# FFN1 of four tiles in pairs, x resident between statistics and normalization, split rings for x, and h2 held on chip, in a Hymba-style decoder layer

## Chip, cores and metric

One Trainium2 chip, eight cores. Each core computes four of the 32 sequences, with no exchange between cores. The time of a run is the device time of the slowest core. "A die" is cores 0 to 3 or cores 4 to 7. Some executions fell into a slow state, in which one die or both were granted a lower TensorE clock (in the kernel before, medians of 0.80 to 0.91 on the worse die, against 0.92 to 0.93 in its fast runs).

## The reference, cut to what matters

```python
h = h + 0.5 * swiglu(rmsnorm(h, g_ffn1), w_ffn1_gate, w_ffn1_up, w_ffn1_down)   # FFN1 -> h1
u = rmsnorm(h, g_mix)
proj = u @ w_in                                                                # the mixer:
o = concat(rmsnorm(mla_group(...)), rmsnorm(swa_group(...)))                   # two attention groups
h = h + o @ w_o                                                                # -> h2
h = h + 0.5 * swiglu(rmsnorm(h, g_ffn2), w_ffn2_gate, w_ffn2_up, w_ffn2_down)   # FFN2
return rmsnorm(h, g_final)
```

D_MODEL is 1024, D_FF 2816. A core works on 16 tiles of 512 tokens, features on the partitions, so a tile of x, h1 or h2 is eight blocks of 128x512 float32, 256 KB each (2.1 MB).

## The kernel before

The program writes its operations in any order, each with a priority `v`. A list scheduler with a model of durations then fixes the order of every engine, and semaphores follow from the data. So the order on an engine is fixed before the run. Four streams are interleaved: FFN1 and FFN2 tile by tile, the mixer of one tile spread between them, and at the start the "background", which converts the weights of the mixer and FFN2 from float32 to bf16 in device memory. FFN1's weights are converted while the first two tiles ("J") use them.

```python
NX = 3
X = [sb(f"X{i}", [128, T], F32)[0] for i in range(NX)]      # one ring for x, h1 and h2
...
phases = [("J", 0, 2 * ff)]                                  # tiles 0 and 1 share each weight piece
for n in range(2, look): phases.append(("F1", n, ff))        # look = 4
for n in range(1, NT + 1):
    phases.append(("F2", n - 1, ff))
    if n + look - 1 < NT: phases.append(("F1", n + look - 1, ff))
...
def load_x(src, key, dv=-8.0):
    i, t = xr.next()
    k.dma(f"x{i}", t[:], src, ...)
...
if ph == "F1":                                               # x twice through the ring
    sc.v = vmap(f0 - 45.0); x_stats(n, rsF)                  # 8 loads, squares, sum on GpSimd
    sc.v = vmap(f0 - 20.0); make_uF(n, uF, rsF)              # 8 loads, uF = x * g * rs
...
# end of the mixer
    i, t = load_x(h1_s[n, dc], ("h1", n, dc))
    k.tt("dve", t[:], PS[bk][:], t[:], ALU.add)              # h2
    st.add(t[:])
    k.dma(f"xs{i}", h2_s[n, dc], t[:], ...)
for c in range(8):
    _, t = load_x(h2_s[n, c], ("h2", n, c))                  # h2 again, for FFN2
    k.stt(uF[:, c, :], t[:], gcol("f2", c), rsH[:], ALU.mult, ALU.mult)
```

FFN1 and FFN2 have a gate/up phase G (352 matmuls of 128x128x512 a tile) and a down phase D (176). A "round" is FFN2 of one tile, FFN1 of another and a mixer; there are twelve, then a tail of FFN2 and mixers without FFN1.

The softmax here doesn't subtract the row's maximum and nothing guards it: scores larger than these inputs give would overflow.

## Time and profile before

| | before |
|---|---|
| median of 3 first runs | 6023.84 us (6017.51 to 6049.1) |
| profiled fast run | 6063 us on its slowest core (core 5) |
| FFN2 of tile 0 starts (core 5) | 837 us |
| a round, mean of twelve | 359.5 us |
| tail, from FFN2 of tile 12 on | 912 us |
| bytes moved | 1083.54 MB |

The prediction shows the lines. They are read thus: in the view by stretches the share of PE busy time says how full the bounding engine is, and the granted clock says what its work cost; matmuls times 0.206 us (the price in a phase without waits at clock 1.00) is what the stretch would need. The rest is loss. The 0.61, 0.54 and 1.00 that the prediction sets side by side are granted clocks of its views; its half clock is a granted 0.50, as the trace of this run (core 5) has it from 456 to 504 us (8 matmuls, PE busy for 3.9 us) and from 2442 to 2458, in the gap of 21.7 us. In the waits, sb_uF is the normalized input of an FFN, sb_sqb the sum of squares that the statistics matmul reads, sb_W a weight piece, sb_tb the buffers of the tanh chain; sb_stJ and sb_stB are the staging buffers of FFN1's weights and of the background, sb_obB the background's converted pieces.

### The profile page before, as it was taken

The page shows a single profiled execution, that of the slowest core. Times are in us where ns is not written, and L with a number is a line of the kernel's source. Part 1 is how long each engine was busy: PE and PEld are TensorE (multiplying, and loading weights), DVE is VectorE, ACT ScalarE, POOL GpSimd, SP SyncE. Part 2 cuts the span into 40 slices and gives each one's busy share as a digit, 9 for nine tenths or more (in the row PEclk, how much of TensorE's full clock was granted, in tenths as well). Part 3 has the DMA queues.
Part 4 walks back from the last instruction along what each step waited for, and adds up shares of the span by engine and source line. Part 5 has one row for each costly group of instructions (what it writes and reads, how often), then busy time and mean ns, then how long its engine had stood idle before and what let it go on. Part 6 is the DMA issues. An engine that isn't in the chain of part 4 may idle for free.

```text
span 6063.0 us, 78231 instructions; the slowest of 8 cores (5933.8 to 6063.0 us)
## 1 busy us (share of the span) xinstructions
PE 5233.1 (86%) x23152; PEld 2234.1 (37%) x23152; DVE 2374.5 (39%) x3418; ACT 2514.0 (41%) x4215; POOL 1222.3 (20%) x1511
## 2 busy tenths in 40 slices
PE   1976889899898899889898888989989889889878
PEld 0422334343333334334343333434334343334333
DVE  0313434435434444533435353343533444443432
ACT  1102424445353433525455242434535343646551
POOL 3441212111111211212111121211111121121210
PEclk9988899999998999999999999999999999989887
DMA  9996565644545555564644656555464555463534
GB/s 277 302 307 188 163 211 169 193 157 154 192 151 187 169 186 169 159 205 152 184 144 132 209 165 211 169 188 161 148 199 151 186 170 187 134 195 117 156 117 138
DMA packets 426072, 1083.54 MB, mean 179 GB/s; under 512 B 47424, under 2 KB 52032, under 8 KB 425536
## 3 DMA queue, kind: packets, MB, share of 16 engines
q1 hardware_dynamic: 425664, 1078.54, 56.3%
q8 instruction: 202, 3.31, 0.2%
q14 instruction: 206, 1.69, 0.1%
HBM read 933.52 MB, written 144.83 MB: 178 GB/s over the span
## 4 chain that ended last, share of the span: by engine, by line
PE 61%; DMA 23%; DVE 5%; ACT 4%; issue 3%; POOL 2%; SPq 2%; DVEq 0%; ACTq 0%; POOLq 0%
PE ps L315 61%; DMA sb_stB_100<-wgu 2%; SPq L364 2%; DMA sb_X_63<-h2s 2%; DMA h1s<-sb_X_63 2%; DMA sb_X_62<-xT 2%; DMA sb_X_62<-h1s 2%; DMA h1s<-sb_X_62 1%; DMA sb_X_61<-h1s 1%; DMA sb_X_63<-h1s 1%; DMA sb_X_63<-xT 1%; DMA h2s<-sb_X_61 1%; DMA h2s<-sb_X_62 1%; DVE sb_HB L340 1%; DMA sb_X_61<-xT 1%
## 5 line engine op out<-in xcount | busy, mean ns | idle before, releaser
L315 PE MATMUL ps<-sb_uF,sb_W_66 128*128 128x512 bf16 x2720 | 684.0, 397 | 160.7 <-DVE sb_uF L340 137.6
L315 PE MATMUL ps<-sb_uF,sb_W_64 128*128 128x512 bf16 x2736 | 672.6, 389 | 79.4 <-DVE sb_uF L340 74.3
L315 PE MATMUL ps<-sb_uF,sb_W_65 128*128 128x512 bf16 x2736 | 661.6, 389 | 49.6 <-DVE sb_tb_78 L340 40.0
L315 PE MATMUL ps<-sb_uF,sb_W_67 128*128 128x512 bf16 x2720 | 661.2, 393 | 30.1 <-POOL sb_W_67 L334 8.5
L323 ACT ACT_TABLE_LOAD x269 | 345.1, 1283 | 458.1 <-PE ps L315 444.1
L315 PE MATMUL ps<-sb_QT,sb_KT 96*128 96x512 bf16 (+3 forms) x1280 | 434.2, 369 | 78.9 <-ACT sb_PT_75 L323 19.7
L340 DVE SCALAR_TENSOR_TENSOR sb_tb_78<-sb_tb_78,ps 128x512 f32<-128x512 f32 x352 | 241.7, 687 | 607.8 <-ACT sb_tb_78 L323 607.3
L315 PEld LDWEIGHTS ps<-sb_uF,sb_W_66 128*128 128x128 bf16 x2720 | 266.9, 100 | 524.3 <-issue 249.1
L340 DVE SCALAR_TENSOR_TENSOR sb_tb_79<-sb_tb_79,ps 128x512 f32<-128x512 f32 x352 | 241.6, 686 | 550.6 <-ACT sb_tb_79 L323 549.5
L315 PEld LDWEIGHTS ps<-sb_uF,sb_W_64 128*128 128x128 bf16 x2736 | 266.3, 99 | 427.4 <-issue 143.0
L323 ACT ACTIVATE sb_tb_79<-ps 128x512 f32<-128x512 f32 x352 | 210.1, 597 | 504.9 <-PE ps L315 503.7
L315 PEld LDWEIGHTS ps<-sb_uF,sb_W_65 128*128 128x128 bf16 x2736 | 267.7, 99 | 391.6 <-issue 108.0
L315 PEld LDWEIGHTS ps<-sb_uF,sb_W_67 128*128 128x128 bf16 x2720 | 269.8, 100 | 378.8 <-issue 95.8
L323 ACT ACTIVATE sb_tb_78<-ps 128x512 f32<-128x512 f32 x352 | 210.1, 597 | 473.1 <-PE ps L315 471.9
L315 PE MATMUL ps<-sb_act,sb_W_66 128*128 128x512 bf16 x1364 | 338.1, 392 | 18.8 <-DVE sb_X_63 L340 8.5
L315 PE MATMUL ps<-sb_act,sb_W_65 128*128 128x512 bf16 x1364 | 329.2, 389 | 19.2 <-DMA sb_W_65<-wd1s 13.1
L315 PE MATMUL ps<-sb_act,sb_W_67 128*128 128x512 bf16 x1364 | 327.3, 388 | 20.0 <-POOL sb_W_67 L334 15.8
L315 PE MATMUL ps<-sb_act,sb_W_64 128*128 128x512 bf16 x1364 | 331.6, 385 | 14.6 <-DMA sb_W_64<-wd1s 8.1
L348 POOL TENSOR_TENSOR sb_sqa_83<-sb_sqa_83,sb_sq_81 128x512 f32<-128x512 f32 x88 | 112.0, 1272 | 964.8 <-ACT sb_sq_81 L323 963.3
L348 DVE TENSOR_TENSOR sb_act<-sb_tb_78,ps 128x512 bf16<-128x512 f32 x352 | 241.4, 686 | 144.7 <-PE ps L315 139.8
L348 POOL TENSOR_TENSOR sb_sqa_82<-sb_sqa_82,sb_sq_80 128x512 f32<-128x512 f32 x139 | 183.0, 1317 | 531.0 <-ACT sb_sq_80 L323 520.0
L348 DVE TENSOR_TENSOR sb_act<-sb_tb_79,ps 128x512 bf16<-128x512 f32 x330 | 226.4, 686 | 141.7 <-PE ps L315 136.3
(200 smaller groups left out, 6998.7 us busy)
## 6 DMA issues: line engine op xcount, KB each, us to landing
sb_W_66<-wgu2s SPq DMA_DIRECT2D x94, 512.0 KB, 3.9
sb_W_67<-wgu2s SPq DMA_DIRECT2D x94, 512.0 KB, 3.9
sb_W_64<-wgu1s SPq DMA_DIRECT2D x83, 512.0 KB, 3.3
sb_W_65<-wgu1s SPq DMA_DIRECT2D x83, 512.0 KB, 3.2
sb_W_64<-wgu2s SPq DMA_DIRECT2D x82, 512.0 KB, 4.0
sb_W_65<-wgu2s SPq DMA_DIRECT2D x82, 512.0 KB, 3.7
sb_C_69<-wms SPq DMA_DIRECT2D x72, 512.0 KB, 4.5
sb_C_68<-wms SPq DMA_DIRECT2D x72, 512.0 KB, 4.5
```

The lines of the kernel that those rows point to most:

```text
L315: inst = nc.tensor.matmul(out, lhsT=lt, rhs=r, start=st, stop=sp, skip_group_check=True)
L323: return self.sc.op("act", lambda: nc.scalar.activation(out=out, in_=in_, func=func, scale=scale, **kw), 0.2 + nfree(out) / 1200, rd, [out ...
L340: return self.sc.op("dve", lambda: nc.vector.scalar_tensor_tensor(out=out, in0=in0, scalar=scalar, in1=in1, op0=op0, op1=op1), (nfree(out) ...
L348: return self.sc.op(eng, lambda: e.tensor_tensor(out=out, in0=in0, in1=in1, op=op), (n + 151) / 960 if eng == "dve" else 0.25 + n * 2.6 / ...
L364: return self.sc.op("sp", lambda: nc.sync.dma_start(out=out, in_=in_), 0.07, reads, writes, dma=sem, nbytes=nbytes, dv=dv)
```

## The change

The intent is to fill PE at the start and at the borders of the phases: tiles 2 and 3 share weight pieces as tiles 0 and 1 do; x is loaded once into HB (free between FFN2's output and its next down phase) and stays for statistics and normalization; FFN and mixer have rings of their own; h2 stays in Nb and Db until FFN2 has normalized it. The diff, cut to its core:

```diff
-        X = [sb(f"X{i}", [128, T], F32)[0] for i in range(NX)]
+        XF = [sb(f"XF{i}", [128, T], F32)[0] for i in range(3)]
+        XM = [sb(f"XM{i}", [128, T], F32)[0] for i in range(2)]
-        phases = [("J", 0, 2 * ff)]
-        for n in range(2, look):
-            phases.append(("F1", n, ff))
+        phases = [("J", (0, 1), 2 * ff), ("P", (2, 3), 2 * ff)]
+        hc = [Nb[:, c, :] for c in range(4)] + [Db[:, c, :] for c in range(4)]
+        def prep_thread():
+                if ph == "P":                       # tiles 2, 3, during down of tiles 0, 1
+                    load_tile(n[0], HBl, "hb"); tile_stats(HBl, rsF, None)   # squares summed on PE
+                    make_u(uFl, HBl, rsF, "f1") ...
+                elif ph == "F1":
+                    yield vmap(f0 - ff + 14.0)      # during FFN2's gate/up
+                    load_tile(n, HBl, "hb")
+                    ... st.add(HBl[c])
+                    yield vmap(f0 - fdn - 1.0)      # during FFN2's down
+                    make_u(uFl, HBl, rsF, "f1")
 # J: x of tiles 0 and 1 resident (xJ), statistics on PE, residual added in place
-                        x_stats(tt_, ...); make_uF(tt_, ...)
+                        load_tile(q, xJ[q], f"xj{q}"); tile_stats(...); make_u(...)
 # end of the mixer
-                    k.tt("dve", t[:], PS[bk][:], t[:], ALU.add)
+                    k.tt("dve", hc[dc], PS[bk][:], t[:], ALU.add)
-                _, t = load_x(h2_s[n, c], ("h2", n, c))
-                k.stt(uF[:, c, :], t[:], gcol("f2", c), rsH[:], ALU.mult, ALU.mult)
+                k.stt(uF[:, c, :], hc[c], gcol("f2", c), rsH[:], ALU.mult, ALU.mult)
 # background: two staging buffers for three, later target times
```

Besides: the scheduler's model of DMA goes from 340 to 310 GB/s, a mixer's place in the order begins 4 us later, and act2 and uF2 are tracked block by block.

## The prediction

> **What bounds the kernel now.** I read the page first (PE busy, the 40 slices), then cut the span at the phases of the kernel with the view by stretches, then asked for PE's waits in two of these stretches, then for the chain of waits inside one round. The page:
>
> ```profile
> PE 5233.1 (86%) x23152; PEld 2234.1 (37%) x23152; DVE 2374.5 (39%) x3418; ACT 2514.0 (41%) x4215; POOL 1222.3 (20%) x1511
> ...
> PE   1976889899898899889898888989989889889878
> ...
> PEclk9988899999998999999999999999999999989887
> DMA  9996565644545555564644656555464555463534
> ```
>
> PE is the bound, but 830 us of the span it is idle, and the clock is below full. The first three slices (450 us) are full of DMA and thin in PE; everything else is PE at 80 to 90% with DMA half busy. So there are two problems, and I look at them apart.
>
> Phase borders come from the timeline of PE: a gate/up phase (G) runs from the first to the last matmul that reads sb_uF against a weight tile, a down phase (D) likewise with sb_act. Columns: stretch and its length, then busy us (and instructions) of PE, PEld, DVE, ACT, POOL, the granted clock, DMA share, GB/s.
>
> ```profile
> 0.00:61.10 61.10, 0.63 (x2) 0.18 (x2) 0.93 (x3) 9.70 (x13) 26.81 (x29) 1.00 0.96 294
> 61.10:317.90 256.80, 169.67 (x706) 71.12 (x707) 71.83 (x102) 36.37 (x57) 100.25 (x97) 0.95 0.97 290
> 317.90:451.10 133.20, 94.53 (x353) 37.49 (x350) 10.36 (x15) 8.82 (x14) 62.51 (x71) 0.82 0.98 307
> 451.10:497.70 46.60, 1.74 (x4) 0.32 (x4) 2.38 (x4) 11.30 (x17) 23.69 (x23) 0.54 0.84 258
> 497.70:837.00 339.30, 304.77 (x1348) 130.59 (x1349) 140.62 (x204) 120.96 (x205) 61.40 (x81) 0.92 0.59 178
> 837.00:5151.40 4314.40, 3883.35 (x17365) 1665.62 (x17364) 1788.23 (x2561) 1887.61 (x3162) 794.81 (x996) 0.94 0.54 173
> 5151.40:6063.00 911.60, 778.43 (x3381) 328.73 (x3379) 360.13 (x530) 439.28 (x747) 152.84 (x216) 0.89 0.45 143
> ```
>
> They are: start; G and D of the first two tiles (weights converted on the way); the wait before tile 2; FFN1 of tiles 2 and 3 with the first mixer; twelve rounds of FFN2, FFN1 and a mixer; the tail of FFN2 and mixers. Next, one round (D of FFN2, the gap after it, G and D of FFN1, G of FFN2):
>
> ```profile
> 2387.30:2436.30 49.00, 49.00 (x238) 22.84 (x237) 7.97 (x12) 24.42 (x46) 12.55 (x22) 1.00 0.53 166
> 2436.30:2458.00 21.70, 12.87 (x40) 3.71 (x38) 11.82 (x13) 16.68 (x32) 14.13 (x16) 0.61 0.69 231
> 2458.00:2570.20 112.20, 103.87 (x448) 42.93 (x448) 63.17 (x96) 61.51 (x100) 13.09 (x16) 0.95 0.42 132
> 2570.20:2627.00 56.80, 48.35 (x212) 20.70 (x211) 10.68 (x16) 9.42 (x14) 12.64 (x10) 0.94 0.79 247
> 2627.00:2745.20 118.20, 108.31 (x512) 48.30 (x511) 54.76 (x81) 44.33 (x70) 14.93 (x23) 0.96 0.53 173
> ```
>
> The first of these is a phase without loss: 49.0 us for 238 matmuls, 0.206 us each. I use this as the price of PE's work. At it, 23152 matmuls are 4769 us; the loss is 2413 x 0.206 = 497 of 837 us up to FFN2 of tile 0 (340 lost), 17365 x 0.206 = 3577 of 4314 in the rounds (737 lost, 61 a round), 696 of 912 in the tail (216 lost). In the round shown: the gap 13.5, G of FFN1 20, D of FFN1 13, G of FFN2 13. The chain inside D of FFN1 names the cause:
>
> ```profile
> 2562.39 5.98 DMA h2s<-sb_X_62
> 2568.46 0.04 issue
> 2568.49 4.97 DMA sb_X_62<-h1s
> ...
> 2574.33 4.96 DMA h2s<-sb_X_62
> ...
> 2580.78 4.85 DMA h2s<-sb_X_61
> 2585.72 0.04 issue
> 2585.76 4.45 DMA sb_X_61<-h1s
> ```
>
> A buffer of the one ring of three X tiles is stored, waited for, loaded, stored again; x for statistics, x for normalization, x for the residual, h1 twice and h2 twice all pass through it.
>
> [...] 0.61 in the 21.7 us gap, 0.54 in the 46.6 us one, 1.00 in the phase without waits. So closing a gap pays more than its length. [...] The X tiles' loads here take 2.0 us at least and 4.2 in the median to land, 256 KB each; a store and a reload are two of these in series. [...] in the full stretches I see 290 to 307, which I take as the ceiling. [...]
>
> **The change, part by part.**
>
> (1) Start and first two tiles. Before, the second tile's x goes three times through the ring with loads that wait behind the weights, and PE, in order, stands at its statistics matmul (the longest such wait on sb_sqb is 57.8 us). In D, 16 residual tiles each hold an X buffer for a load and a store of 10 to 15 us: 16/3 x 25 = 133 us, just what D takes against 352 x 0.206 = 73. After, x is resident, statistics accumulate on PE, and there is no ring here. G should start near 25 us. What is left is DMA: 22 pieces read as float32 and written as bf16 (1.57 MB each) are 34.6 MB; before, with the other conversion (the background) beside it, they got some 170 to 180 GB/s of 300; now the background has two buffers for three, so I take 180: 34.6/180 = 192 us, G ends at about 220. D needs 17.3 + 4.2 MB: at about 200 GB/s 105 us, the end near 325 (before 451). The background's later target dates hardly slow it: they only rank work that is ready, and its loads are limited by buffers.
>
> (2) Pair of tiles 2 and 3. Its inputs are made during D of the first pair: the gap of 46.6 and the one of 28 between tiles 2 and 3 go. Weights are loaded once: 17.3 MB less. PE: 1056 FFN matmuls and the first mixer's, 1348 x 0.206 = 278 us. The background has 37 MB left (120 in all less what went before), together with weights, h1 and mixer loads about 68 MB, 230 us at 295 GB/s: beside PE, but with long latencies. With 35 us lost: FFN2 of tile 0 starts near 325 + 278 + 35 = 640 for 837. **Gain 197.**
>
> (3) Rounds. x for FFN1 lies in HB before D of FFN2, its square sums are made in G, and normalization (8 x 0.75 us on DVE) in D beside PE. So the gap closes: 12 of its 13.5 us lost. G of FFN1 loses its wait for sb_uF and the half clock at its start, about 6, but the final normalization and output of the last tile (8 operations, 9.5 us in the timeline with what runs between) now compete with its first tanh chains: minus 4. D of FFN1: the mixer's h1 has its own ring and h2 needs no buffer, so the wait for the sum over h2 (7.0 us here) goes: 6. G of FFN2: uF comes straight from h2 on the chip: the wait for sb_uF (5.7) and half of the half-clock time: 6. Less 1 for the next mixer's start, which must wait until h2 has been read. Sum 25 a round, x12: **gain 300.** As a check, PE's idle time in the rounds is 4314 - 3883 = 431 us, a list of its waits there begins with
>
> ```profile
> PE ps L315 <- DVE sb_uF L340: 135.4, 65, 6.0
> ```
>
> and clock 0.94 means 12% at half clock, 518 us, about 140 us of work lost if PE was half busy then. 300 of these 570 is what I claim; exponentials (about 100 us of small waits) and tanh chains stay.
>
> (4) Tail. Here only h2 changes: gaps of 42.4 (50 matmuls, 32 lost) and 11.7 before the last two FFN2 phases are half mixer latency, half round trips of h2. I take 45. **Gain 45.**
>
> (5) Bytes: 38 MB of x, 17 of weights, 34 of h2 go, 1083 to about 995 MB. Outside the front DMA is half busy; that itself gains nothing.
>
> Sum: 6024 - 197 - 300 - 45 = 5482; plus 33 for what I have not seen (order of engines fixed in advance on a model, DVE bursts), 5515.
>
> **Rivals.** (a) The front stays bound by DMA and the saving there is only bytes: 8.4 MB of x, 28 us, plus the closed gaps; FFN2 would start near 740. For it: DMA at 96 to 98% until 451. Against it: PE stood on statistics and residual buffers, while the background ran ahead and finished early. Then about 5615. (b) The gap is filled but a new wait comes in its place: the tanh chain waits behind the final normalization, or PE stands at the statistics matmul of the next x. DVE at 41% in the rounds speaks against it, its strict order for it. If half of the rounds' gain is lost: 5665. [...] (d) Ordinary luck in the other direction: half-clock time falls by more than its share, 5430.
>
> **Range and chances.** The parts have spreads of about 60 (front), 70 (rounds), 25 (tail), and 50 for the clock: together about 110. I set 5400 to 5680. Faster by over 2% means below 5903; even the front alone with a third of the rounds gets there: 0.96, within 2% 0.03, slower 0.01.
>
> **What would show it.** Right: first gate/up matmul before 35 us; first D near 100 us, not 133; FFN2 of tile 0 from 600 to 690; no gap between D of FFN2 and G of FFN1; waits for sb_uF in the rounds under 40 us; clock in the rounds 0.96 or more; rounds near 335 us; 995 MB. Wrong: rounds above 348 us, waits for sb_tb grown to over 150 us, a first D that is still above 125 us, or long stretches granted 0.81.

## The result, and the profile after

The first four timed runs of the changed kernel took 5756.63 to 5964.79 us, median 5795.43, beside 6036.47 for the kernel before. All four were slow: at least one die was granted less clock (medians of 0.85 to 0.89, against 0.96 to 0.98 on the dies of the fast runs). Two more executions were fast, 5373.62 and 5420.63 us. The ratio of fast runs to fast runs is **0.895** (0.8841 to 0.906). A ratio here is the mean time of one kernel's fast runs over that of the other's of the same rounds, so not quite the ratio of the medians quoted. At 0.895 of 6024 the time is some 5390 us: faster than predicted (5515) and just below the low end of my range (5400), which lies inside the interval (5326 to 5458).

In the profiled run of that set the two dies differ (mean clock and median span of each die), and the profile's page shows the disturbed one. Below the dies stands one dense stretch of its slowest core:

```profile
die 0 (median of its cores): 5745.1 us, clock 0.891
die 1 (median of its cores): 5360.2 us, clock 0.977
```

```profile
4500.00:4700.00 200.00, 197.43 (x776) 82.75 (x790) 88.09 (x134) 88.90 (x150) 33.68 (x54) 0.81 0.42 133
```

PE is 99% busy and granted 0.81: that is not the change. The unaltered kernel was run again (e1) and gave a profile with both dies fast. From its page:

```profile
PE 5047.5 (93%) x23180; PEld 2219.0 (41%) x23180; DVE 2305.8 (43%) x3418; ACT 2603.4 (48%) x4289; POOL 1175.6 (22%) x1483
...
PE   7779999999999999999999999999999999989878
...
PEclk9989999999999999999999999999999999999989
DMA  9998554755447565554645555565554656364434
```

PE rose from 86% to 93% and the clock digits are 9 nearly throughout. The same seven stretches as before (start; G and D of tiles 0 and 1; G and D of tiles 2 and 3; the twelve rounds; the tail; there is no wait of 46.6 us between the pairs to list any more):

```profile
0.00:26.20 26.20, 6.30 (x12) 1.18 (x12) 1.19 (x4) 9.92 (x16) 4.80 (x9) 1.00 0.89 244
26.20:218.20 192.00, 165.80 (x718) 70.42 (x717) 74.90 (x106) 41.45 (x64) 74.22 (x72) 0.96 0.99 305
218.20:374.10 155.90, 103.09 (x361) 40.10 (x362) 22.45 (x29) 16.75 (x26) 63.55 (x66) 0.79 0.98 286
374.10:583.90 209.80, 197.81 (x921) 87.04 (x920) 99.10 (x148) 96.60 (x158) 68.88 (x103) 0.98 0.74 228
583.90:676.30 92.40, 92.40 (x428) 41.55 (x427) 32.61 (x46) 30.06 (x48) 32.56 (x24) 1.00 0.67 208
676.30:4569.00 3892.70, 3739.18 (x17365) 1655.92 (x17364) 1723.07 (x2568) 1982.59 (x3241) 781.40 (x996) 0.99 0.57 179
4569.00:5412.20 843.20, 742.90 (x3382) 322.78 (x3379) 352.45 (x521) 426.04 (x736) 150.17 (x215) 0.94 0.46 145
```

The 651 us between the two profiles (6063 and 5412) lie in the front (837 to 676: 161), the rounds (4314 to 3893: 422) and the tail (912 to 843: 69). Core 5 of the kernel before was on the die with less clock (0.924, the other 0.933); against its core 0 (table below) the three are 143, 395 and 47. In the rounds PE's idle time fell by 277 us (431 to 154) and its busy time, for as many matmuls, by 144 (3883 to 3739). The third line is the surprise: down of the first pair takes 156 us, not less than the 133 before. One round, the counterpart of the one in the prediction (D of FFN2, what is left of the gap, G and D of FFN1, G of FFN2):

```profile
2083.30:2132.10 48.80, 48.80 (x237) 22.72 (x236) 13.26 (x20) 24.19 (x46) 12.51 (x21) 1.00 0.56 167
2132.10:2133.30 1.20, 0.99 (x7) 0.36 (x5) 0.69 (x1) 0.73 (x3) 0.00 (x0) 1.00 0.87 355
2133.30:2248.80 115.50, 108.53 (x481) 45.85 (x480) 64.15 (x97) 80.06 (x128) 15.98 (x25) 0.96 0.45 144
2249.50:2300.00 50.50, 45.84 (x211) 20.32 (x210) 16.33 (x24) 10.65 (x16) 15.44 (x12) 1.00 0.89 280
2300.00:2404.00 104.00, 103.47 (x501) 47.25 (x500) 48.38 (x73) 49.88 (x76) 22.08 (x26) 1.00 0.56 183
```

The gap of 21.7 us is 1.2. G of FFN2 is 104.0 us for 501 matmuls, which at 0.206 is 103.2: no loss left. PE's waits for sb_uF in all twelve rounds, 135.4 us before, are in the first run's undisturbed core 4

```profile
PE ps L314 <- DVE sb_uF L339: 3.9, 14, 0.3
```

### The profile page after: what moved, and what is told of

Read it like the earlier page. It is cut to its first block, busy times and chain, and to the rows that moved or that the text cites.

```text
span 5755.6 us, 76628 instructions; the slowest of 8 cores (5328.8 to 5755.6 us)
## 1 busy us (share of the span) xinstructions
PE 5430.7 (94%) x22720; PEld 2327.1 (40%) x23180; DVE 2307.1 (40%) x3418; ACT 2612.3 (45%) x4289; POOL 1176.3 (20%) x1483
## 2 busy tenths in 40 slices
DMA packets 381423, 994.84 MB, mean 173 GB/s; under 512 B 42464, under 2 KB 47072, under 8 KB 380896
## 4 chain that ended last, share of the span: by engine, by line
PE 81%; DMA 7%; DVE 3%; ACT 3%; issue 3%; POOL 2%; SPq 1%; DVEq 0%; POOLq 0%; ACTq 0%
PE ps L314 81%; DMA sb_stB_125<-wm 2%; SPq L363 1%; DMA sb_XM_64<-h1s 1%; DMA sb_XM_65<-h1s 1%; DVE sb_uF L339 1%; ACT L322 1%; DMA sb_stB_125<-wgu 0%; DVE sb_uO L339 0%; DMA sb_C_71<-wms 0%; DVE sb_HB L339 0%; DMA sb_W_68<-wd1s 0%; POOL sb_KT L333 0%; DMA h1s<-sb_XF_61 0%; ACT sb_Db L322 0%
## 5 line engine op out<-in xcount | busy, mean ns | idle before, releaser
L314 PE MATMUL ps<-sb_uF,sb_W_68 128*128 128x512 bf16 x2585 | 689.5, 411 | 27.5 <-DVE sb_tb_81 L339 9.7
L314 PE MATMUL ps<-sb_uF,sb_W_67 128*128 128x512 bf16 x2588 | 681.4, 411 | 35.1 <-DVE sb_tb_80 L339 22.4
L314 PE MATMUL ps<-sb_uF,sb_W_66 128*128 128x512 bf16 x2589 | 674.2, 408 | 19.5 <-DVE sb_tb_81 L339 7.3
L314 PE MATMUL ps<-sb_uF,sb_W_69 128*128 128x512 bf16 x2580 | 670.9, 408 | 11.9 <-POOL sb_W_69 L333 4.5
L314 PE MATMUL ps<-sb_act,sb_W_68 128*128 128x512 bf16 x1295 | 345.2, 410 | 24.8 <-POOL sb_W_68 L333 16.0
L314 PE MATMUL ps<-sb_act,sb_W_66 128*128 128x512 bf16 x1290 | 346.0, 412 | 14.9 <-POOL sb_W_66 L333 11.1
L314 PE MATMUL ps<-sb_act,sb_W_69 128*128 128x512 bf16 x1297 | 335.5, 407 | 13.8 <-POOL sb_W_69 L333 6.9
L314 PE MATMUL ps<-sb_act,sb_W_67 128*128 128x512 bf16 x1294 | 334.9, 406 | 8.7 <-POOL sb_W_67 L333 6.3
L347 DVE TENSOR_TENSOR sb_act<-sb_tb_80,ps 128x512 bf16<-128x512 f32 x352 | 241.6, 686 | 191.4 <-PE ps L314 184.3
L347 DVE TENSOR_TENSOR sb_act<-sb_tb_81,ps 128x512 bf16<-128x512 f32 x308 | 211.2, 686 | 140.6 <-PE ps L314 132.9
L347 POOL TENSOR_TENSOR sb_sqa_84<-sb_sqa_84,sb_sq_83 128x512 f32<-128x512 f32 x124 | 158.9, 1281 | 501.3 <-ACT sb_sq_83 L322 497.7
L347 POOL TENSOR_TENSOR sb_sqa_84<-sb_sqa_84,sb_sq_82 128x512 f32<-128x512 f32 x128 | 163.4, 1277 | 324.0 <-ACT sb_sq_82 L322 313.2
```

The source lines that it names most:

```text
L314: inst = nc.tensor.matmul(out, lhsT=lt, rhs=r, start=st, stop=sp, skip_group_check=True)
L347: return self.sc.op(eng, lambda: e.tensor_tensor(out=out, in0=in0, in1=in1, op=op), (n + 151) / 960 if eng == "dve" else 0.25 + n * 2.6 / ...
```

## Experiments

Each was timed beside the kernel before. "Start" is where FFN2 of tile 0 starts, "round" the mean of the twelve, both from the phase borders in the profile of a fast run (its slowest core). e1 to e4 ran on one chip, e5 to e8 on a second, e9 to e11 on a third; fast runs of the kernel before took 6036 to 6055, 6009 to 6078 and 6040 to 6055 us there, so a difference of half a percent between these sets shows nothing. Rounds and phases come from one profile each.

| run | start | round | tail | ratio to before |
|---|---|---|---|---|
| before (core 5; core 0) | 837; 819 | 359.5; 357.3 | 912; 890 | 1 |
| e1 the change again | 676 | 324.4 | 843 | 0.894 (own division: 5413.24 and 5396.39 over 6054.92 and 6036.1) |
| e2 before + x resident (core 6; core 0) | 840; 842 | 342.4; 342.6 | 942; 889 | 0.9696 (0.9582 to 0.981) |
| e3 change, x twice | 663 | 343.0 | 843 | 0.9312 (0.9236 to 0.9388) |
| e4 change, h2 reloaded, mixer ring of 2 | 673 | 340.5 | 889 | one fast run, 5649.07 |
| e5 the same, one ring of 5 | 659 | 331.3 | 854 | 0.9094 (0.9012 to 0.9177) |
| e6 change, one ring of 3 | 668 | 328.8 | 841 | 0.9039 (0.8977 to 0.9101) |
| e7 change, no pair | 670 | 322.1 | 842 | 0.8914 (0.8835 to 0.8994) |
| e8 paced background | 624 | 322.9 | 839 | 0.887 (0.881 to 0.893) |
| e9 paced, no pair | 633 | 324.7 | 838 | 0.8868 (0.8833 to 0.8902) |
| e10 first x through the ring | 726 | 324.6 | 842 | 0.9038 (0.9011 to 0.9066) |
| e11 paced, FFN1 kept for the tail | 638 | | | 0.8903 (0.8858 to 0.8948) |

**e1.** No edit.

> The changed kernel once more, unaltered, on the same chip as the next three, for a profile with both dies undisturbed if the chip allows. Expected: fast runs at 0.895 of before, some 5375 to 5420 us; a round of FFN2, FFN1 and mixer 323 us on an undisturbed die (359.5 before), the twelve rounds starting near 664 us. [...]

Two of four runs were fast, 5413.24 and 5396.39 us, as expected.

**e2.** The kernel before, with x resident alone:

```diff
-                    if ph == "F1":
+                    if ph == "F1" and n < 4:
                         sc.v = vmap(f0 - 45.0); x_stats(n, rsF) ...
+        def prep_thread():          # n >= 4: load x into HB, sums during G, uF during D of FFN2
```

> The kernel before with one part of the change alone: from tile 4 on, x is loaded once into HB, its sums of squares made during FFN2's gate/up and its normalization during FFN2's down; one ring of three X buffers, single tiles and h2 through memory stay. Theory 1 (the gap of 22 us between FFN2 and FFN1 is the largest single loss of a round, and x residency closes it): about 20 us a round come back, 240 in all, 5785 us, ratio 0.96. Theory 2 (the common ring is the disease, and what is taken off it helps all its other users too): 30 us a round or more, 5660 us, ratio 0.94, with the waits in FFN1's down phase and at FFN2's start falling as well.

A round fell by 17.1 us (core 5 of before as the base; 14.7 between the two cores 0), near theory 1's 20 and far from theory 2's 30. The gap before FFN1 went from 22.7 to 0.7 us and G of FFN1 grew from 111.0 to 115.6, because the mixer matmuls of the gap moved into it. G of FFN2 stayed at 117.8 and D of FFN1 at 54.8 (118.7 and 54.1 before): nothing was given to the ring's other users. The tail of 942 us is the clock's: this core was granted 0.84 there; core 0 of the same run, on the die with more clock (0.92 over its last 912 us), has 889, as core 0 of before has 890. A gap that is 22.0 us shorter was thus worth 15 to 17 us and not more than its length: PE had been working in it (40 matmuls of the mixer in the one shown).

**e3.** The change with x loaded twice again, through its own ring.

```diff
-                elif ph == "F1":    # prep_thread: x into HB
+                    if ph == "F1":  # at the phase itself, as before: 8 loads + 8 loads through XF
+                        sc.v = vmap(f0 - 45.0) ... sc.v = vmap(f0 - 20.0) ...
```

> The changed kernel with that part undone: FFN1 from tile 4 on loads x twice, for statistics and for normalization, through the FFN ring, at the moments of the kernel before. Rings stay split, pairs and h2 on the chip stay. Theory 1: the gap comes back nearly whole, since FFN2's residual loads hold the same ring until its down phase ends: 18 us a round, +215 us, 5605 us, ratio 0.93. Theory 2: with the mixer off this ring three buffers are enough, the gap is under 8 us, ratio 0.91 or lower.

The gap came back whole, 23.9 us, the round rose by 18.6. Taking the mixer off the ring does not close the gap; residency does. Added to the one kernel and taken from the other, the part is worth 15 to 19 us a round: some 175 to 225 us. Here too the gap is dearer in length (23.2 us) than in time.

**e4 and e5.** h2 stored and loaded again, first with the mixer's ring of two, then with all five buffers in one ring.

```diff
-                    k.tt("dve", hc[dc], PS[bk][:], t[:], ALU.add)
+                    k.tt("dve", t[:], PS[bk][:], t[:], ALU.add)      # and stored from t
-                k.stt(uF[:, c, :], hc[c], gcol("f2", c), rsH[:], ...)
+                _, t = load_x(xmr, "xm", h2_s[n, c], ("h2", n, c))
+                k.stt(uF[:, c, :], t[:], gcol("f2", c), rsH[:], ...)
 # e5 besides:
-        xfr = Ring(XF)
-        xmr = Ring(XM)
+        xfr = Ring(XF + XM)
+        xmr = xfr
```

> The changed kernel with h2 stored from the mixer's ring of two buffers and loaded again for FFN2's normalization, as before the change. Theory 1: FFN2's start waits for h2 again, 6 us a round and its share of half clock, and the tail loses 25: +100 us, 5490 us, ratio 0.912. Rival: a round trip of h2 runs beside FFN1's down phase and is hidden now that FFN does not share the ring: within 20 us of the changed kernel, ratio 0.898 or lower. If two buffers are too few it is more than 12 us a round, +170 us, ratio 0.923.

> The run with h2 reloaded cost 16 us a round (340.5 against 324.4), but its mixer had a ring of only two buffers. Here h2 is stored and loaded again as there, and all five X buffers form one common ring, so no load of h2 lacks a buffer. If the cost was the missing buffers, a round is 326 to 330 us and the time within 1.5% of the changed kernel (ratio to before about 0.905). If the cost is the round trip of store and reload itself between the mixer's end and FFN2, the round stays at 337 us or more and the ratio near 0.93.

e4 cost 16.1 us a round, the case of too few buffers (by one fast run); the tail rose by 46, of which 35 went with five buffers (e5). PE's longest waits in its rounds, and then the first in those of e5:

```profile
PE ps L314 <- DVE sb_uF L339: 100.0, 63, 7.1
PE ps L314 <- POOL sb_sqb L347: 63.9, 24, 6.0
```

```profile
PE ps L314 <- DVE sb_uF L339: 74.0, 34, 5.0
```

With five buffers a round is 331.3, between my two cases: of the 16 us, 9 were the ring of two and 7 are left to the round trip, which five buffers did not remove (the wait for sb_uF is still 74.0 us). (e5 has one common ring besides, whose own cost with five buffers I did not measure.) What h2 on the chip is worth therefore depends on the buffers it saves: it lets the mixer live with two. Without it, five buffers for all cost some 94 us in rounds and tail, two for the mixer 239.

**e6.** One ring of three for all, x resident and h2 on the chip.

```diff
-        xmr = Ring(XM)
+        xmr = xfr
```

> The changed kernel with one ring of three X buffers for FFN residuals and mixer together, as before; x stays resident, h2 stays on the chip, pairs stay. My prediction gave the mixer's own ring 6 us a round: then 330 us, +75 us in all, ratio 0.908. Rival from the runs so far (x residency 17 to 19 us, h2 on the chip 16 to 17 us, which sum to the whole 35): the split is worth nothing once x and h2 have left the ring: 325 us a round, ratio 0.896.

4.4 us a round, 53 in all: close to the 6 I had given it. (The run also has three buffers where the change has five in two rings; one ring of five with h2 on the chip was not run, so the split and the number are not told apart.) But the loss does not lie where I had put it. D of FFN1 stayed at 51.6 us (52.0 in e1); the time stands between D of FFN1 and G of FFN2, in six gaps of 7 to 10 us.

This run shows one thing more. Its tail has gaps of 2, 6 and 3 us before its last three FFN2 phases, the tail of e1 has 11, 39 and 57, and both take the same time (841 and 843). In the tail a gap tells where the mixer's work stands in the order; it is not a loss of its length.

**e7.** Tiles 2 and 3 one after the other.

```diff
-        phases = [("J", (0, 1), 2 * ff), ("P", (2, 3), 2 * ff)]
+        phases = [("J", (0, 1), 2 * ff), ("F1", 2, ff), ("F1", 3, ff)]
```

> The changed kernel with tiles 2 and 3 one after the other, each loading its own weight pieces, inputs prepared ahead as elsewhere. Theory: the front gained by the closed waits before and between these tiles and by an earlier end of the first pair, not by weights shared; PE bounds this stretch, so FFN2 of tile 0 starts 0 to 20 us later (664 to 676 before), ratio 0.896 to 0.899. Rival: with the background still converting, 17 MB more at 300 GB/s are 57 us in a stretch bound by DMA: the start near 725, ratio 0.905.

The start, 670 us, lies between the 664 and 676 of the two profiles with pairs, and the ratio is not worse. (The edit also makes the input of tile 2 alone during the first down phase, so this phase is a little lighter than with pairs.) The 17 MB saved do show as bytes: this stretch with single tiles, in the view by stretches,

```profile
353.00:670.30 317.30, 291.78 (x1350) 127.78 (x1349) 141.73 (x206) 141.44 (x224) 115.73 (x133) 0.99 0.89 276
```

moves 276 GB/s, against 228 and 208 with pairs, and PE, 92% busy at clock 0.99 here and 96% with pairs (e1), is the bound in both. The stretch itself is 9 to 15 us longer than in the two profiles with pairs (308 and 302), but it starts earlier. The first words of the change's description name a part whose worth these runs can't tell from nothing.

**e8.** The background held to a pace: each staging load waits for a gate/up step.

```diff
+                        sc.lw[("pace", ph, lc)] = len(sc.ops) - 1          # after each gate/up pair
-                    yield v0
-                    v0 += (235.0 - 120.0) / 22 if idx < 11 else 3.9
+                    ph_, lc_ = ("J", hh * 20 // 22) if hh < 22 else ("P", min((hh - 22) * 20 // 76, 20))
+                    yield vmap(...)
-                    k.dma(f"sb{j}", s_[:, 0:h], src[...], [], ...)
+                    k.dma(f"sb{j}", s_[:, 0:h], src[...], [("pace", ph_, lc_)], ...)
```

> The changed kernel with the background conversion held to a pace: 22 of its 98 half pieces are spread over gate/up of the first pair, none in its down phase, the rest over gate/up of the second pair, each load waiting for a step of FFN1. It tests why the first down phase still takes 139 to 156 us where I predicted 105. Theory: the background takes the bandwidth and GpSimd's order there; without it this phase needs 26 MB, 85 to 95 us, and it shrinks to under 100. FFN2 of tile 0 then starts near 630 (the same bytes must go later beside PE), total 35 us less, ratio 0.889. Rival: the phase is held by something of its own (conversion copies behind each other on GpSimd, stores of the converted weights): it stays above 125 us, and the bytes put off slow the second pair, so the start is later than 690 and the ratio 0.90 or more.

The stretches (as above, from the first pair's G on: G, D, G and D of the pairs):

```profile
25.60:204.80 179.20, 162.34 (x719) 70.09 (x719) 73.05 (x105) 41.47 (x64) 68.50 (x67) 0.97 0.97 303
204.80:299.40 94.60, 83.29 (x362) 35.73 (x360) 20.76 (x30) 16.75 (x26) 39.41 (x43) 0.95 0.88 280
299.40:520.10 220.70, 199.75 (x923) 87.27 (x921) 98.94 (x146) 97.71 (x159) 80.98 (x105) 0.97 0.85 260
520.10:624.50 104.40, 93.40 (x426) 40.75 (x424) 33.38 (x44) 27.52 (x45) 44.38 (x42) 1.00 0.93 289
```

D of the first pair fell from 156 to 95 us. The second pair grew from 302 to 325 by the bytes put off, and FFN2 of tile 0 starts at 624. PE's wait for the converted weights in that D, in e1 and then in e8:

```profile
PE ps L314 <- POOL sb_W L333: 47.9, 10, 10.9
```

```profile
PE ps L314 <- POOL sb_W L333: 8.1, 3, 4.1
```

So the background held this phase. By bandwidth or by its place in GpSimd's order, where a copy that waits for its load stands before FFN1's copies? The run takes away both, and the traces show both at work. By bandwidth: D moved 44.6 MB in e1 (155.9 us at 286 GB/s), of which 17.3 are 22 loads and 22 stores of the background issued in it, and 26.5 MB in e8 (94.6 us at 280), at nearly the same rate. By order: GpSimd in this D of e1 waited longer for the background's loads than for FFN1's own,

```profile
POOL sb_obB L333 <- DMA sb_stB<-wgu: 42.0, 13, 6.0
POOL sb_W L333 <- DMA sb_stJ<-wd: 18.5, 12, 4.0
```

The share of each is not known. With e9, this version is the fastest: four fast runs of 5338.99 to 5349.37 us, 0.887.

**e9.** e8 with single tiles 2 and 3.

> The paced background (FFN2 of tile 0 at 624 us, ratio 0.887) with tiles 2 and 3 one after the other. Without pacing the pair was worth nothing (670 us against 664 to 676). With pacing the second stretch moves 260 to 289 GB/s, so shared weights should count there: 17 MB at 290 GB/s are 60 us, of which I expect half to show, the start at 650 to 660. If it stays below 635, shared weights are worth nothing in either case; above 680, all 17 MB count.

Start at 633, 9 us later than with pairs, ratio 0.8868: by my own mark, below 635, shared weights are worth nothing here either, or no more than these 9 us. It costs DMA, not time: the view by stretches has 289 to 290 GB/s over 300 to 640 us.

**e10.** x of tiles 0 and 1 through the ring again, statistics on GpSimd.

```diff
-                        load_tile(q, xJ[q], f"xj{q}"); tile_stats(...); make_u(...)
+                        8 x (load_x(xfr, ...); st.add(t[:])); 8 x (load_x(xfr, ...); k.stt(...))
-                            f1_resid(q, dc, bk, sts[q], (xJ[q], q))
+                            f1_resid(q, dc, bk, sts[q])
```

> The changed kernel with x of the first two tiles loaded three times through the FFN ring and its squares summed on GpSimd, as before; all else stays. Theory: this part alone made the first gate/up start at 26 instead of 62 us and end at 217 instead of 313: both come back, and FFN2 of tile 0 starts 85 to 100 us later than 664 to 676, near 765, ratio 0.911. The first down phase, whose length I had put down to this ring, stays where it is (130 to 160 us) in either case. Rival: the end of the first pair is set by the bytes in any case, and only the first 35 us come back: start near 705.

Gate/up started at 58 us and ended at 282; the start of FFN2 came 50 to 62 us later, between theory and rival. Before the change this gate/up ended at 318: the other 36 us are not x's, and what else in the change gave them (the background's later dates and fewer buffers, say) was not tested. The waits that came back at the head of PE's list in this first G:

```profile
PE ps L314 <- DVE sb_uF L339: 34.6, 8, 12.3
PE ps L314 <- POOL sb_sqb L347: 13.6, 1, 13.6
```

Its D took 153 us, with the ring, as e1's took 156 without. The second pair then ran in 291 us against 302: with more of the background done by then, some of the loss was given back.

**e11.** The paced kernel without FFN1 in rounds 4 and 8, so that it still stands beside mixers 13 and 14.

```diff
-            if n + 3 < NT:
-                phases.append(("F1", n + 3, ff))
+            if nxt < NT and n not in (4, 8):
+                phases.append(("F1", nxt, ff)); nxt += 1
```

> A try at a better version, with the paced background: FFN1 is left out of rounds 4 and 8, whose mixers are the shortest, so that FFN1 still stands beside the mixers of rounds 13 and 14. The changed kernel's tail (843 us, 697 at 0.206 us a matmul) has gaps of 10, 36 and 54 us before its FFN2 phases, where mixers run without FFN1 beside them. Expected: the first two of these close, 35 us less in all than the paced kernel, ratio 0.881. Rival: rounds 4 and 8 get such gaps in their place and nothing is won (0.886 to 0.888).

The first two gaps (12 and 37 us in the paced kernel's profile) closed and the last one grew from 57 to 73. From the start of FFN2 to the end it took 4761 us, the paced kernel 4714: no gain. By the ratios (0.8903, and 0.887 and 0.8868 for e8 and e9) the intervals overlap, so it is not shown to be worse. The rival's form (gaps like those in rounds 4 and 8) isn't seen either: elsewhere no border has a gap over 4 us. Of the 47 us, 26 are PE's busy time for as many matmuls (4497 and 4471 us); the cause I did not settle. That closing the gaps won nothing agrees with e6, whose tail without gaps was as long.

## Why the prediction was right or wrong, step by step

**Direction and mechanism: right.** PE waits at phase borders and the half clock that came with them (0.50 from 2442 to 2458 us in the gap shown) were the loss. Both went: the clock in the rounds rose from 0.94 to 0.99, that is, taking half clock as the only other state as the prediction did, from 518 to about 78 us at half clock (2 x 0.01 x 3893). Read in steps of 1 us, the rounds of before (core 5) have 489 steps of 4314 granted 0.50 and 3721 granted 1.00, those of the first run of the change (core 4) 57 and 3778 of 3879. One step of it was wrong: that closing a gap pays more than its length. 22.0 us of gap less were worth 15 to 17 a round (e2), 23.2 more cost 18.6 (e3). My sum had not relied on it (12 for a gap of 21.7).

**(3) Rounds: right in kind, the sum too small, 300 for 422.** By the same accounting in the example round: gap and G of FFN1 lost 33.8 us before (133.9 us, 486 matmuls) and 16.7 after (117.4 us, 489): 17 came back, I had 14 (12 + 6 - 4). D of FFN1: 13.1 and 7.0, so 6 as I had in this round; but the mean over twelve fell only from 54.1 to 52.0. G of FFN2: 12.7 and 0.8, so 12 came back where I had 5. This last is the mis-sized term. I counted only the listed wait for sb_uF and half of the half-clock time; e4 and e5 show that h2's round trip and the buffers it held were worth some 7 and 9 us a round. In the means of twelve rounds, gap and G of FFN1 fell by 18.4 us, D of FFN1 by 2.1, G of FFN2 with the gap before it by 14.5.

**The split ring: right size, wrong place.** 4.4 us for 6, with two buffers more, but at FFN2's start and not in D of FFN1 (e6).

**The fear of a new wait (rival b): not borne out.** PE's waits for sb_tb in the rounds were 58.7 us before (39.6 and 19.1) and 48.9 in e1.

**(1) The first pair: half right.** Start at 26 us for 25, end of G at 218 for 220. But D was 156 (139 in the first run) for 105, and the step before it was wrong: I had put D's 133 us in the kernel before down to the ring of X buffers, because 16/3 x 25 us came out at just this number. The ring went and D stayed; e10 brought the ring back and D stayed again; e8 took the background away and D fell to 95. A sum that fits the duration exactly was no evidence. What was mis-sized are the bytes of this D: I had 21.5 MB at 200 GB/s, leaving the rest of the queue to the background; it moved 44.6 MB at 286, 17.3 of them the background's, and 26.5 without it. One of my signs of being wrong, "a first D that is still above 125 us", came true.

**(2) The second pair: its price right (302 for 313), its reason partly wrong.** The gaps of 46.6 and 28 us closed because inputs were prepared ahead; the sharing of weights gave nothing that these runs can tell (e7, e9). Front in all: 161 for 197, the difference being that D.

**(4) Tail: the number right, the reason wrong.** 69 in the profiles of core 5 and e1; core 0 of before, which had a tail of 890 us, gives 47. I had 45, for the two gaps of 42.4 and 11.7 us before the last two FFN2 phases. They did not close: in e1 they are 38.5 and 57.3, and with the one before them (4.2, then 11.3) the gaps grew from 58 to 107 us, while the FFN2 phases between them got shorter. The agreement of the gaps' sum with the result is luck. With h2 reloaded the gain goes (e4 loses 46, e5 with five buffers 11), so it hangs on h2's buffers more than on its round trip; through which waits was not followed.

**(5) Bytes: right.** 994.84 MB for 995.

**The clock.** The slow state struck about half of all runs of either kernel (18 of 33 before, 32 of 63 of the change and its variants), and in it the change took 5757 to 5965 us in its first set, the kernel before 6484. It is not caused by the change as far as these runs tell.

## What to carry to other kernels

When one ring of buffers serves several streams, ask of each stream whether its data could stay where it is instead of passing through: undone singly, residency of x for FFN1 cost some 223 us and residency of h2 some 240 (94 where it had more buffers), one ring of three for two rings of five in all 53, and single weights nothing that could be measured: those bytes were moved beside a PE that was 92% busy (e7). The fixed gap at a phase border closed when the next phase's input was made during the last one. Don't count a gap at its length: PE may be working in it, and the work moves elsewhere when it closes (22 us of gap for 15 to 17 us of time in the rounds, nothing in the tail). Where a background stream competes with a critical one, tie it to the critical one's steps; here, later target times and a buffer fewer left the phase at 139 to 156 us (133 before), the tie brought 95.

## What the traces show besides

- The clock. In the fast runs of e1 eight cores, with PE 93% busy on the slowest, kept a mean clock of 0.973 to 0.977 over 5400 us. In the slow run profiled first die 0 shows 0.81 (core 0, 4500 to 4700 us, PE 99% busy), but even there not for the whole load: cores 0 and 1 were granted 0.99 from 676 to 2876 us of their traces and 0.81 from 3050 to 5276, cores 2 and 3 of the same die 0.81 and then 0.98 to 0.99, with PE 95 to 99% busy in all of these (the traces have no common start, so whether the halves fell together can't be told). The profiled fast run of the kernel before has 0.81 too, at its end (core 5, 5930 to 6045 us, PE 100% busy).
- Loads. In the kernel before, 512 KB loads of FFN1's gate and up weights into their staging buffers took 16.3 to 17.1 us in the median in the first 318 us (DMA 96 to 97% busy), and 512 KB loads of converted weights, nearly all later, 3.2 to 4.0 us (DMA 54% busy in the rounds).
- The background. Left to get ahead of FFN1's conversion, it cost 61 us in one phase (156 and 95 us, e1 and e8; 139 in the first run of the change), of which 52 remained at the end of the front (676 and 624).
